# Where the first up pair's weight parts are made and how the last squares are added, in a fused hybrid decoder layer on one core

## The chip, the cores and the metric

The kernel runs on one core of one Trainium2 chip. The time is the device time of one launch in microseconds; a kernel is judged by the median of several launches. The profile is one launch taken by the hardware profiler. The engines are named as the profile names them: PE is the matrix engine (PEld its weight loads), DVE the vector engine, ACT the scalar engine, POOL is GpSimd, SP the engine that only issues transfers. "SPq", "ACTq" and "POOLq" are transfers issued from these engines' queues.

## What is computed

One decoder layer over 1024 positions of width 1024, in float32: a norm, two attention branches, a gated merge of the branches, an output product (the mixing layer) with a residual, then a norm and a gated MLP with a short convolution, a residual and a last norm. The parts that matter here:

```python
xn = rmsnorm(x, norm_mix_w[l])
proj = xn @ w_in[l]
...
merged = jax.nn.sigmoid(g_da) * (y_da @ w_br_da[l]) + jax.nn.sigmoid(g_sw) * (y_sw @ w_br_sw[l])
x = x + merged @ w_mix_out[l]
xn = rmsnorm(x, norm_ffn_w[l])
x = x + conv_ffn(xn, w_up[l], conv_w[l], conv_b[l], w_down[l])
```

## The kernel before

**Numbers in two parts.** Every operand of a product is held as a high part (a rounded copy, made on ACT, L252 or L150) and a low part (source minus high part, made on DVE, L254 or L152). A product is three matmuls: high by high, high by low, low by high. So each weight tile of 128 by 1024 costs one load on SP, one cast on ACT and one subtraction on DVE before PE can use it. `raw` (three buffers) takes the loads, `wh` and `wl` (two buffers each) the parts; in the up projection `sh`, `sl` (three each) and `rv` are used beside them.

**Fast products.** The input projection, the mixing layer, the up and the down projection each form a block product by seven half-size products (Strassen's scheme in Winograd's form): P1 to P7 over operands A11, A12, S1 to S4, A22 of the weights and B11, B21, T1 to T4, B22 of the activations. The sums among weights for the mixing layer are made in memory during the input projection: copies on SP and accumulating transfers on POOL, by a generator `sums_of` that is advanced some steps for each of nine weight pairs (L568). After it `sums_up` (L106) does the same for one up pair, j = 1, into the tensor `ud`, in eight steps.

**Attention, then the merge.** The branch outputs lie in the tensor `yd` and the gates' inputs in `gd`. In `rest` (L896) eight rows of `yd` are loaded (`yr`, L909) and cut into parts `yh`, `yl`; then a loop over m = 0 to 7 does one block row of the merge: load two gate rows (`gr`, four buffers, so those of m+2 can be loaded only when those of m are used up), scale them on POOL (L925), take the sigmoid on ACT (L932), run 48 matmuls on PE into `sc` and `g`, multiply on DVE (L941, L943), and add the two branches into `mr[:, m]` on POOL (L951; the last two on DVE). Rows of `mr` are cut into the parts `x` (and `m22`, for B22) by `split` (L966, L967). The order on each engine is made by a scheduler from the order of the code and `issue_after` ties; an engine runs its instructions strictly in that order.

**Splitting in the merge.** The generator `ahead_parts` (L136), advanced twice in each turn of the merge, loads four tiles (half of the mixing weight, and both tiles of the up pair j = 0), makes that pair's sums on DVE, makes high parts on ACT and low parts on DVE, and stores both parts to memory: `md4` for the mixing layer's last stage, `ud0` for the up pair j = 0. They come back later as finished parts: `md4` through `load_halves` (L117) in stage P4, `ud0` through `pre_pair` (L126) after stage P7.

**The mixing layer** (`mix`, L975) runs the stages P1, P2, P5, P6, P3, P7, P4 in two halves each, numbered i = 0 to 13, of 24 matmuls each (L1117). The weights of half i+1 are fetched at half i. After each half the results are added to the residual rows `xm` on DVE, and a table `due` lists, by half, which operations prepare the up projection's activations: scales and casts on ACT, sums and low parts on DVE. It also holds the squares for the second norm: each row is squared on ACT (L1024) into `sqs` or `rv`, and the squares are summed in `rstd` by POOL. The last four go by an accumulating transfer, the others by an addition:

```python
if m > 3 and hf == 0:
    nc.gpsimd.dma_start(a, sq, accum_op=ALU.add)
else:
    nc.gpsimd.tensor_tensor(a, a, sq, ALU.add)
```

**The up projection** (`hidden`, L1157) takes 22 pairs of seven products of 12 matmuls each (L1154). For j = 0 six products come first (B11, T1, B22, T3, T2, B21), then the column sums of `rstd` on PE (L281), the last product (T4), the first two products of j = 1, and the spreading of the norm's factor (L296). `recombine` adds the products up; for a pair whose sums came by `sums_up` its signs differ (`pre`).

Of the kernel before, what the change touches and what calls it, by code (L numbers as in the profile page):

```python
# [27 lines left out]
RAW = 3  # L28
HP, HPB, HR = 7, 13, 11
# [16 lines left out]
class Trunk:  # L46
# [27 lines left out]
    def ahead(self, n):  # L74
        while len(self.wq) < n and self.wsrc and (self.wsrc[0][1] != "pair" or self.uw):
# [10 lines left out]
            elif nk == "halves":  # L86
                self.wq.append(self.load_halves(src, "raw" if src is self.md4[0] else None))
            else:
                self.wq.append(self.load_w(src, nk, *eng))
# [16 lines left out]
    def sums_up(self):  # L106

        nc, d = self.nc, self.ud
        row = lambda j, r: self.w_up[j].rearrange("p k c -> p (k c)")[:, r * H2:(r + 1) * H2]
        copy = lambda n, src: nc.sync.dma_start(d[:, n], src)  # L110
        add = lambda n, src: nc.gpsimd.dma_start(d[:, n], src, accum_op=ALU.add)
        for f, n, src in ((copy, 0, row(1 + NF, 0)), (copy, 2, row(1 + NF, 0)), (add, 0, row(1 + NF, 1)), (add, 2, row(1, 0)),
                          (copy, 1, d[:, 0]), (add, 1, row(1, 0)), (copy, 3, d[:, 1]), (add, 3, row(1, 1))):
            f(n, src)
            yield

    def load_halves(self, src, tag=None, pool=None, tags=("wh", "wl"), shape=[P, KC, P]):  # L117

        r = []
        for d, t in zip(src, tags):  # L120
            x = self.tl(self.wp, shape, tag, F32R, bufs=RAW) if tag else self.tl(pool or self.wp, shape, t, F32R)
            self.sync = self.nc.sync.dma_start(x.bitcast(F32).rearrange("p a k c -> p (a k c)" if len(shape) == 4 else "p k c -> p (k c)"), d).ins
            r.append(x)
        return r

    def pre_pair(self):  # L126

        w, shape = {}, [P, 2, 4, P]
        for i, n in enumerate((("A11", "A12"), ("S1", "S2"), ("S3", "S4"))):
            hi, lo = self.load_halves(self.ud0[i], None, self.uw if i else self.wp, ("sh", "sl") if i else ("wh", "wl"), shape)  # L130
            w.update({name: (hi[:, a], lo[:, a]) for a, name in enumerate(n)})
        x, = self.load_halves(self.ud0[3], None, self.uw, ("sh",), shape)
        w["A22"] = x[:, 0], x[:, 1]
        return w

    def ahead_parts(self, pool):  # L136


        nc, tt = self.nc, self.nc.vector.tensor_tensor
        late = []  # L140

        def load(src):
            t = self.tl(pool, [P, T], "yr")
            nc.sync.dma_start(t.rearrange("p (m k c) -> p m k c", m=src.shape[1], k=src.shape[2]) if len(src.shape) == 4 else t.rearrange("p (k c) -> p k c", k=KC), src)
            return t

        def cut(t, hi, lo, n=T):
            h = self.tl(pool, [P, T], "yh", F32R, bufs=1)
            x, r = t[:, T - n:], h[:, :n]
            nc.scalar.copy(r, x)  # L150
            nc.scalar.dma_start(hi, r.bitcast(F32))
            tt(x.bitcast(F32R), x, r.bitcast(F32), ALU.subtract)  # L152
            late.append(lambda: nc.sync.dma_start(lo, x))

        def sums(g, v):
            q = lambda t, i: t[:, i * H2:(i + 1) * H2]
            a, b = (self.tl(pool, [P, T], "yr") for _ in range(2))
            tt(q(a, 0), q(v, 0), q(v, 1), ALU.add)
            tt(q(a, 1), q(a, 0), q(g, 0), ALU.subtract)
            tt(q(b, 0), q(g, 0), q(v, 0), ALU.subtract)  # L160
# [20 lines left out]
        for m in range(KC):  # L181
            steps = plan(m)
            while late:
                late.pop(0)()
# [1377 lines left out]
```

## Time and profile before

| | |
|---|---|
| median of 3 runs | 1345.48 us (1343.78 to 1346.31) |
| the profiled execution | 1345.87 us, its span 1344.0 us |
| PE busy | 1311.3 us (98%), granted clock 0.986 |
| DVE, ACT, POOL busy | 1069.9, 639.9, 502.3 us |
| stages, from the trace | projection to 240 us, attention to 497, merge to 608, mixing to 686, up projection to 1121, down to the end |

A busy share is a mean over stages with different limits, so the stages are looked at one by one: how long PE stood still in each, at what clock it ran, and what ended its waits. Durations of single instructions are in microseconds (ns where marked); "idle before" in brackets is the time that the engine stood still ahead of the row and what ended it.

### The profile page before, as it was taken

The numbers are of one execution on the slowest core, as the hardware profiler recorded it, in microseconds if no ns is written. First come the engines' busy times: TensorE is split into PE (matmuls) and PEld (weight loads), VectorE is DVE, ScalarE is ACT, GpSimd is POOL, SyncE is SP. The second block draws the span as 40 slices with busy tenths as digits, with TensorE's granted clock in tenths as the row PEclk, the third lists the DMA queues.
The fourth block names the chain that finished last, engine by engine and source line by source line (L and its number), as shares of the span: only waits on it lengthen the run. The fifth ranks groups of instructions, "written<-read, shape, count | busy, mean of one in ns | idle before, by whom it ended". The sixth has DMA issues, their size and how long they took to land.

```text
span 1344.0 us, 17329 instructions
## 1 busy us (share of the span) xinstructions
PE 1311.3 (98%) x6162; PEld 1090.2 (81%) x6162; DVE 1069.9 (80%) x1516; ACT 639.9 (48%) x1010; POOL 502.3 (37%) x399
## 2 busy tenths in 40 slices
PE   9999999999999999799998999999999999999997
PEld 7888888888888878677876888888888888888886
DVE  8846684388898964557787999999999999896865
ACT  9432232376676764234654443343334335554643
POOL 0448762010101006653244666676657642000002
PEclk9999999999999999898998999999999999999998
DMA  8357776966552157759594534663636237953534
GB/s 296 130 165 214 225 213 163 276 178 172 157 134 89 61 178 255 221 191 317 155 287 154 182 126 131 169 203 101 201 121 153 86 102 244 319 197 114 167 96 145
DMA packets 87318, 238.21 MB, mean 177 GB/s; under 512 B 9665, under 2 KB 17473, under 8 KB 86977
## 3 DMA queue, kind: packets, MB, share of 16 engines
q1 hardware_dynamic: 64848, 193.86, 43.2%
q0 software_dynamic: 8640, 23.07, 10.2%
q10 hardware_dynamic: 13744, 20.19, 4.1%
q8 instruction: 48, 0.79, 0.3%
q14 instruction: 38, 0.30, 0.1%
HBM read 176.27 MB, written 88.08 MB: 197 GB/s over the span
## 4 chain that ended last, share of the span: by engine, by line
PE 85%; DMA 5%; POOL 4%; issue 3%; ACT 1%; DVE 1%; SPq 1%; POOLq 0%; ACTq 0%; DVEq 0%
PE t L1154 43%; PE y L1375 9%; PE d L1375 7%; PE m L1117 5%; PE g L273 3%; PE g L274 3%; PE g L275 3%; PE sc L766 3%; POOL gr L925 2%; DMA gr<-gd 2%; POOL mr L951 1%; DMA rstd<-rv 1%; PE t L782 1%; PE t L885 1%; PE sc L854 1%
## 5 line engine op out<-in xcount | busy, mean ns | idle before, releaser
L254 DVE TENSOR_TENSOR wl<-raw,wh 128x1024 fp32r<-128x1024 f32 (+2 forms) x89 | 94.3, 1060 | 56.2 <-ACT wh L252 46.6
L252 ACT CAST wh<-raw 128x1024 fp32r<-128x1024 f32 (+2 forms) x89 | 78.3, 881 | 88.9 <-PE y L1375 47.6
L1154 PE MATMUL t<-T,sh 128*128 128x512 f32 x364 | 113.1, 395 | 0.0
L1305 POOL TENSOR_TENSOR us<-us,rstd 128x1024 f32<-128x1024 f32 x42 | 93.6, 2303 | 50.3 <-DVE us L599 32.5
L290 POOL TENSOR_TENSOR rs<-ms,mhalf 128x8 f32<-128x8 f32 (+2 forms) x9 | 13.3, 1478 | 236.9 <-DVE ms L288 230.7
L217 POOL TENSOR_TENSOR sf<-rv 128x512 f32<-128x512 f32 x29 | 59.5, 2052 | 97.4 <-DMA rv<-in_w_up 51.2
L231 ACT CAST sh<-sf 128x1024 fp32r<-128x1024 f32 x58 | 60.7, 1047 | 67.5 <-PE t L1154 32.7
L1319 ACT ACTIVATE c<-us,vecs 128x1024 f32<-128x1024 f32 x44 | 54.7, 1247 | 70.6 <-POOL us L1305 67.4
L233 DVE TENSOR_TENSOR sl<-sf,sh 128x1024 fp32r<-128x1024 f32 x58 | 78.5, 1354 | 12.0 <-ACT sh L231 11.9
L1154 PE MATMUL t<-x,wh 128*128 128x512 f32 x248 | 82.2, 389 | 0.0
L1154 PEld LDWEIGHTS t<-T,sh 128*128 128x128 f32 x364 | 69.4, 191 | 14.6
L1322 DVE SCALAR_TENSOR_TENSOR c<-us,vecs,c 128x1024 f32<-128x1024 f32 x44 | 73.3, 1698 | 0.1
L273 PE MATMUL g<-xh,wh 128*128 128x512 f32 x176 | 71.1, 404 | 1.4 <-ACT g L695 1.4
L274 PE MATMUL g<-x,wh 128*128 128x512 f32 x176 | 70.5, 400 | 0.0
L275 PE MATMUL g<-xh,wl 128*128 128x512 f32 x176 | 70.3, 399 | 0.0
L1154 PE MATMUL t<-x,sh 128*128 128x512 f32 x212 | 68.7, 392 | 0.0
L1154 PE MATMUL t<-T,sl 128*128 128x512 f32 x176 | 68.5, 389 | 0.0
L233 DVE TENSOR_TENSOR wl<-raw,wh 128x1024 fp32r<-128x1024 f32 x29 | 67.7, 2333 | 0.6
L1321 DVE SCALAR_TENSOR_TENSOR c<-us,vecs,c 128x1024 f32<-128x1024 f32 x44 | 65.0, 1511 | 1.7 <-ACT c L1319 1.7
L1375 PE MATMUL y<-h,wh 128*128 128x512 f32 (+1 forms) x224 | 65.3, 375 | 0.0
L219 POOL TENSOR_TENSOR sf<-raw,rv 128x512 f32<-128x512 f32 x29 | 52.2, 1801 | 34.4 <-DVE sl L233 34.4
L770 DVE CUSTOM_DVE_ANT_0 L<-sc,bias 128x128 f32<-128x128 f32 (+7 forms) x64 | 47.7, 752 | 17.5 <-PE sc L766 14.0
(350 smaller groups left out, 3978.4 us busy)
## 6 DMA issues: line engine op xcount, KB each, us to landing
u<-qd SPq DMA_DIRECT2D x72, 256.0 KB, 6.7
raw<-in_w_in SPq DMA_DIRECT2D x22, 512.0 KB, 5.6
hd<-c SPq DMA_DIRECT2D x22, 512.0 KB, 2.6
sdP<-in_w_down POOLq DMA_DIRECT2D x16, 704.0 KB, 9.2
raw<-in_w_up SPq DMA_DIRECT2D x21, 512.0 KB, 5.4
rv<-in_w_up SPq DMA_DIRECT2D x20, 512.0 KB, 3.8
hc<-hd SPq DMA_DIRECT2D x33, 256.0 KB, 5.1
gr<-gd SPq DMA_DIRECT2D x16, 512.0 KB, 6.1
```

The source lines that it names most:

```text
L233: low = nc.vector.tensor_tensor(lo, src, hi.bitcast(F32), ALU.subtract)
L252: self.hi = nc.scalar.copy(wh, raw)
L254: self.lo = (eng or nc.vector).tensor_tensor(wl, raw, wh.bitcast(F32), ALU.subtract)
L273: nc.tensor.matmul(ps, wh[:, kc + o, :], ah, start=first and n == 0, stop=False)
L274: nc.tensor.matmul(ps, wh[:, kc + o, :], al, start=False, stop=False)
L275: nc.tensor.matmul(ps, wl[:, kc + o, :], ah, start=False, stop=last and n == len(kcs) - 1)
L1117: nc.tensor.matmul(ps, v[:, m % 2 * 4 + k, :], x, start=start and k == j == 0, stop=k == 3 and j == 2, skip_group_check=True)
L1154: nc.tensor.matmul(ps, (ah, ah, al)[p][:, k, :], (bh, bl, bh)[p], start=first and n == p == 0, stop=last and p == 2 and n == len(ks) - 1, ...
L1305: i = (nc.vector if m % NF == 0 else nc.gpsimd).tensor_tensor(us[:, 2:], us[:, 2:], self.rstd, ALU.mult)
L1321: nc.vector.scalar_tensor_tensor(c, us[:, 1:T + 1], cw[1], c, ALU.mult, ALU.add)
L1322: nc.vector.scalar_tensor_tensor(c, us[:, 0:T], cw[0], c, ALU.mult, ALU.add)
L1375: nc.tensor.matmul(ps, v[:, k - k0, :], x, start=start and k == i == 0, stop=k == HK - 1 and i == 2, skip_group_check=True)
```

## The change

The merge no longer makes any parts: `ahead_parts`, `load_halves` and `pre_pair` go, with the tensors `md4` and `ud0`. Stage P4's weights are loaded raw and cut like all others. The first up pair, j = 0, now gets its sums as j = 1 did, by `sums_up` during the input projection (NPRE = 2: sixteen steps in place of eight, and 6, 6, 6, then 5 steps for each weight pair in place of 5 and 4). Its parts are made by `part_pair` in the mixing layer: parts 0 and 1 at i = 8 and 9, part 2 at i = 12, part 3 (A22) as the new operation `y3` in the last entry of `due`. They are put where the merged rows `mr` lay: the pool `mp` is closed after stage P3's split, and `uw` is opened there; B22's parts of the merge and T2 share a new pool `zp`. All squares are added by POOL additions. `recombine` takes its other signs for j < 2.

```diff
+NPRE = 2
-            elif nk == "halves":
-                self.wq.append(self.load_halves(src, "raw" if src is self.md4[0] else None))
...
-        copy = lambda n, src: nc.sync.dma_start(d[:, n], src)
-        add = lambda n, src: nc.gpsimd.dma_start(d[:, n], src, accum_op=ALU.add)
+        copy = lambda n, src: lambda j: nc.sync.dma_start(d[j][:, n], src(j))
+        add = lambda n, o, r: lambda j: nc.gpsimd.dma_start(d[j][:, n], row(j + o, r), accum_op=ALU.add)
+        for step in (copy(0, lambda j: row(j + NF, 0)), copy(2, lambda j: row(j + NF, 0)), add(0, NF, 1), add(2, 0, 0),
+                     copy(1, lambda j: d[j][:, 0]), add(1, 0, 0), copy(3, lambda j: d[j][:, 1]), add(3, 0, 1)):
+            for j in range(NPRE):
+                step(j)
+                yield
...
-    def part_pair(self, src, part):
+    def part_pair(self, src, part, first=False):
-        pool, h, l = (self.uw, "sh", "sl") if part in (1, 2) else (self.wp, "wh", "wl")
+        pool, h, l = (self.uw, "sh", "sl") if part in (1, 2) or first else (self.wp, "wh", "wl")
...
-                if name == "P4":
-                    src.append((self.md4[h], "halves"))
-                    continue
-                    m, a = 2 * h, 4 * (name != "P1")
+                    m, a = 2 * h + 4 * (name == "P4"), 4 * (name != "P1")
...
-                for _ in range(5 if j < 4 else 4):
+                for _ in range(6 if j < 3 else 5):
...
-                ahead = self.ahead_parts(yrp)
-                    with tc.issue_after(self.sync):
-                        next(ahead)
-                    with tc.issue_after(self.last.ins):
-                        next(ahead)
...
-            if m > 3 and hf == 0:
-                nc.gpsimd.dma_start(a, sq, accum_op=ALU.add)
-            else:
-                nc.gpsimd.tensor_tensor(a, a, sq, ALU.add)
+            nc.gpsimd.tensor_tensor(a, a, sq, ALU.add)
...
+        def last_part(k):
+            with tc.issue_after(tails[0]), tc.issue_after(tails[1]):
+                w0.update(self.part_pair(pair, k))
+            tails[:] = self.lo.ins, self.hi.ins
...
-                        w = self.next_w(3 if i > 9 else 2)
-                    if i < 11:
+                        w = self.next_w()
+                    if i < 13:
                         tails[:] = self.lo.ins, self.hi.ins
...
                             elif n == 4:
                                 split_m("T4", 4, 0)
+                                mctx.close()
+                                uw = self.hctx.enter_context(tc.tile_pool(name="uw", bufs=3, side="right", reuse_waits="tile"))
+                                pair = self.wsrc.pop([e[1] for e in self.wsrc].index("pair"))[0]
+                    if n == 4 or i == 12:
+                        self.uw = uw
+                        with tc.issue_after(tails[1] if i == 12 else self.hi.ins), tc.issue_after(tails[0] if i == 12 else self.lo.ins):
+                            w0.update(self.part_pair(pair, {8: 0, 9: 1, 12: 2}[i], True))
...
-                    w0 = self.pre_pair()
-                self.recombine(ps, us, tp, 2, self.lo.ins if j == NF - 1 else None, j == 1)
+                self.recombine(ps, us, tp, 2, self.lo.ins if j == NF - 1 else None, j < NPRE)
```

Three places in the order of instructions. The first is SP's queue where the merge begins: the branch rows `yr`, the gate rows `gr` and the branch weights `raw`. Before:

```order
L242 DMA raw_5209<-in_w_br 128x1024
L909 DMA yr_4955<-yd 128x1024
L909 DMA yr_4995<-yd 128x1024
L909 DMA yr_5029<-yd 128x1024
L909 DMA yr_5069<-yd 128x1024
L909 DMA yr_5103<-yd 128x1024
L909 DMA yr_5109<-yd 128x1024
L909 DMA yr_5115<-yd 128x1024
L909 DMA yr_5121<-yd 128x1024
L924 DMA gr_5142<-gd 128x1024
L924 DMA gr_5146<-gd 128x1024
```

and with the change:

```order
L168 DMA raw_5215<-in_w_br 128x1024
L846 DMA gr_5148<-gd 128x1024
L846 DMA gr_5152<-gd 128x1024
L830 DMA yr_5106<-yd 128x1024
L830 DMA yr_5112<-yd 128x1024
L830 DMA yr_5118<-yd 128x1024
L830 DMA yr_5124<-yd 128x1024
L846 DMA gr_5221<-gd 128x1024
L846 DMA gr_5225<-gd 128x1024
L168 DMA raw_5288<-in_w_br 128x1024
```

The first four branch rows moved ahead of these weights, and the first two gate rows (m = 0) ahead of the last four branch rows; those of m = 1 follow these, and no loads of `ahead_parts` come behind them.

The second place is POOL at the end of the mixing layer, where the last squares (`rv`) are added into `rstd` and the operands of T4 into `xm`. Before:

```order
L1027 TENSOR_TENSOR rstd<-rstd,rv_6361 128x512
L1025 DMA rstd<-rv_6362 128x512
L1045 TENSOR_TENSOR xm_5804<-xm_5804,xm_5808 128x512
L1025 DMA rstd<-rv_6362 128x512
L1045 TENSOR_TENSOR xm_5805<-xm_5805,xm_5809 128x512
L1025 DMA rstd<-rv_6361 128x512
L1045 TENSOR_TENSOR xm_5806<-xm_5806,xm_5810 128x512
L1025 DMA rstd<-rv_6361 128x512
L1045 TENSOR_TENSOR xm_5807<-xm_5807,xm_5811 128x512
```

and with the change:

```order
L942 TENSOR_TENSOR rstd<-rstd,rv_6334 128x512 x2
L960 TENSOR_TENSOR xm_5766<-xm_5766,xm_5770 128x512
L960 TENSOR_TENSOR xm_5767<-xm_5767,xm_5771 128x512
L942 TENSOR_TENSOR rstd<-rstd,rv_6333 128x512
L960 TENSOR_TENSOR xm_5768<-xm_5768,xm_5772 128x512
L942 TENSOR_TENSOR rstd<-rstd,rv_6333 128x512
L960 TENSOR_TENSOR xm_5769<-xm_5769,xm_5773 128x512
```

The four transfers became additions; two squares now stand ahead of all T4 sums, and the last still ahead of one.

The third place is DVE from stage P3's second half on: `wl` are the weights' low parts for the next half, `xm` the additions of a half's results. Before:

```order
L1142 TENSOR_TENSOR xm_5805<-xm_5805,m_5828 128x512
L254 TENSOR_TENSOR wl_6219<-raw_6215,wh_6217 128x1024
L1142 TENSOR_TENSOR xm_5806<-xm_5806,m_5829 128x512
L1142 TENSOR_TENSOR xm_5807<-xm_5807,m_5830 128x512
L254 TENSOR_TENSOR wl_6266<-raw_6262,wh_6264 128x1024
L1142 TENSOR_TENSOR xm_5808<-xm_5808,m_5823 128x512
```

and with the change:

```order
L1067 TENSOR_TENSOR xm_5767<-xm_5767,m_5790 128x512
L128 TENSOR_TENSOR sl_6154<-raw_6150,sh_6152 128x1024
L180 TENSOR_TENSOR wl_6191<-raw_6187,wh_6189 128x1024
L128 TENSOR_TENSOR sl_6197<-raw_6193,sh_6195 128x1024
L1067 TENSOR_TENSOR xm_5768<-xm_5768,m_5791 128x512
L1067 TENSOR_TENSOR xm_5769<-xm_5769,m_5792 128x512
L180 TENSOR_TENSOR wl_6236<-raw_6232,wh_6234 128x1024
L1067 TENSOR_TENSOR xm_5770<-xm_5770,m_5785 128x512
```

Two low parts of the first up pair (`sl`) came in, one on each side of the weights for i = 10; further down two more `wl` (stage P4's), one `sl` and one half-size `wl` (A22) are new.

104 lines of the change are left out of this document (19 added, 85 removed), and 2 rows, old and new, of the table due.

## The prediction

> **What bounds the kernel now.** The profiled execution took 1345.87 us with a span of 1344.0; it lies 0.4 above the median. I read first the busy time of each engine by stretches: PE is what the end waits for, so a stage with PE busy throughout at full clock can gain nothing. Columns: from:to, length, busy time and instructions of PE, PEld, DVE, ACT, POOL, then PE's granted clock, the DMA engines' busy share, GB/s.
>
> ```profile
> 497.00:608.00 111.00, 98.47 (x414) 80.12 (x413) 56.83 (x63) 44.88 (x50) 65.04 (x29) 0.95 0.69 225
> 608.00:690.00 82.00, 82.00 (x352) 67.54 (x352) 66.71 (x88) 48.39 (x77) 26.43 (x24) 0.97 0.83 253
> 690.00:730.00 40.00, 32.34 (x132) 26.43 (x131) 25.06 (x29) 14.63 (x23) 19.61 (x17) 0.83 0.69 217
> 730.00:1121.00 391.00, 391.00 (x1727) 323.76 (x1726) 380.85 (x332) 159.11 (x169) 243.73 (x171) 1.00 0.45 138
> ```
>
> The rows are the merge, the mixing layer, the transition to the up projection, and the up projection. The last has no gap and clock 1.00, so it gives PE's pace: 391.00 / 1727 = 0.2264 us a matmul. Against that pace the merge's 414 matmuls need 93.7 us of 98.47 busy (4.7 lost to a lowered clock), and it stood still for 12.5 more. The mixing layer needs 79.7 of 82.00 (2.3 lost). Next, which waits on PE ended these stops (start, duration, engine, line, operation; idle before in brackets), from PE's timeline:
>
> ```profile
> 554.42 0.50 PE L273 MATMUL g<-yh,wh 128*128 128x512 f32 x1 [2.51 <-DVE gr L943]
> 567.35 0.80 PE L275 MATMUL sc<-yh,wl 128*128 128x512 f32 x1 [5.10 <-DVE wl L254]
> 607.58 0.80 PE L1117 MATMUL m<-x,wl 128*128 128x512 f32 x1 [4.92 <-DVE wl L254]
> ```
>
> 2.51 + 5.10 + 4.92 = 12.53: all of the merge's idle time. Merge and mixing together thus hold 12.5 + 4.7 + 2.3 = 19.5 us that a perfect feed would give back. The transition is read from the chain of waits (start, duration, what):
>
> ```profile
> 678.05 6.64 DMA sl<-ud
> 684.72 8.44 DMA rstd<-rv
> 697.55 2.22 DMA rstd<-rv
> 703.73 2.21 DMA rstd<-rv
> 708.93 3.22 DMA rstd<-rv
> 712.20 3.58 PE t L281 x16
> 725.75 0.87 PE t L296 x8
> ```
>
> The column sums (L281) wait for four accumulating transfers in a row. Full-size products in 690 to 730 are 132 less 24 small ones, 108 x 0.2264 = 24.5 us; the column sums at full clock take some 1.7 (an estimate: about half of the 3.58 that they took at a clock near one half) and the spreading 0.9. So 27 of 40 us are work and 13 are lost. In all 19.5 + 13 = 32.5 us can be had, no more.
>
> **Change, merge.** What goes: L150's casts on ACT, L152's cuts on DVE, four sums on DVE, four loads and seven stores of whole or half tiles. I first ask which ring sets the merge's pace. On POOL:
>
> ```profile
> 561.84 2.35 POOL L951 TENSOR_TENSOR mr<-gr,gr 128x1024 f32<-128x1024 f32 x1
> 567.93 5.71 POOL L925 TENSOR_TENSOR gr<-gr,rstd 128x1024 f32<-128x1024 f32 x2 [1.08 <-DMA gr<-gd]
> 573.61 3.37 POOL L951 TENSOR_TENSOR mr<-gr,gr 128x1024 f32<-128x1024 f32 x1
> 586.75 2.40 POOL L925 TENSOR_TENSOR gr<-gr,rstd 128x1024 f32<-128x1024 f32 x1 [3.24 <-DMA gr<-gd]
> 589.10 2.40 POOL L951 TENSOR_TENSOR mr<-gr,gr 128x1024 f32<-128x1024 f32 x1
> 591.53 0.32 SPq L924 DMA_DIRECT2D gr<-gd  x1
> 591.94 0.38 SPq L153 DMA_DIRECT2D ud<-yr  x1
> 592.41 0.38 SPq L924 DMA_DIRECT2D gr<-gd  x1
> 601.71 2.36 POOL L925 TENSOR_TENSOR gr<-gr,rstd 128x1024 f32<-128x1024 f32 x1 [3.61 <-DMA gr<-gd]
> L152 DVE TENSOR_TENSOR yr<-yr,yh 128x1024 fp32r<-128x1024 f32 (+1 forms) x6 | 11.6, 1940 | 5.4 <-ACT yh L150 5.4
> ```
>
> With four `gr` buffers a row's `mr` sum frees the next pair of loads, which then feed two POOL multiplications and a sum. From 564.19 (end of one `mr`) to 576.98 (the next but one's) the ring turned in 12.8 us, with PE needing 48 x 0.2264 = 10.9. It also waited for the second gate row of a pair: 601.71 is 9.3 after its issue at 592.41, behind a store `ud<-yr` of the merge's own parts; the first landed near 595.7, 4.2 after its issue. Without those stores I put the turn at 4.2 for the load, the second row landing while the first is multiplied, 2.4 + 2.4 for the two multiplications and 2.4 for the sum, 11.4, and 0.5 to 1 where a `wl` cut on DVE lengthens the sum as at 573.61 (3.37 for 2.35): about 12. That is still 1.1 over PE's 10.9 for each of some six turns, 6.6 us. Against that stands a lead: the first gate rows are now ahead of four `yr` rows on SP (the first place in the order), four loads, which I take as 6 us. The lead about covers the lag. The two long stops on `wl` go by themselves: the weights' cut no longer stands behind L152 cuts of 1.94 each, nor (at 567.35) behind the `x` part of the row before. I take 16.5 of the 19.5; the bounds are 3 (only the 2.51 stop and its clock, if the gate rows still bind) and 19.5.
>
> **Change, squares and transition.** Four accumulating transfers, 8.44 + 2.22 + 2.21 + 3.22 with waits of 3 to 4.4 between them, become four additions:
>
> ```profile
> L1027 POOL TENSOR_TENSOR rstd<-rstd,sqs 128x512 f32<-128x512 f32 x8 | 12.3, 1544 | 24.4 <-ACT sqs L1142 24.3
> L1025 POOL DMA_DIRECT2D rstd<-rv x4 | 4.2, 1045 | 11.3 <-issue 6.9 <-ACT rv L1142 4.4
> L1045 POOL TENSOR_TENSOR xm<-xm,xm 128x512 f32<-128x512 f32 x4 | 6.4, 1600 | 5.3 <-DVE T L1142 5.3
> 694.01 0.50 PE L1154 MATMUL t<-B,sl 128*128 128x512 f32 x1 [1.82 <-DMA sl<-ud]
> ```
>
> Four at 1.54 and four `xm` sums at 1.60 are 12.6 us of POOL work. The last square's `xm` was ready by the transfer's issue, and POOL's first `xm` sum began at 691.52 on DVE's result; with squares two ahead of the sums and two among them, the last square lies behind at most three sums: 691.5 + 3 x 1.6 + 4 x 1.54 is 702.5. PE's six products of j = 0 end 72 x 0.2264 = 16.3 after the mixing layer's last product, 686.1 + 16.3 = 702.4. So the column sums wait for next to nothing; the 5.83 us that PE now stands still ahead of them go. Also the 1.82 stop goes, since the first pair's parts are now made from the eighth half on and no seven-tile load is due. Of the 13 I keep 4 for T4's low parts, which still come after the `xm` sums, and for a clock lowered once: 9 gained, bounds 3 and 13.
>
> The clock: at 696 to 697, after that stop of 1.82, it was 0.50.
>
> ```profile
> 696.00:697.00 1.00, 1.00 (x4) 0.73 (x3) 0.75 (x1) 1.00 (x3) 0.00 (x0) 0.50 1.03 387
> ```
>
> [...]
>
> **Change, mixing layer.** Added on DVE: five cuts of 128x1024 (two `wl` of P4; parts 0, 1 and 2 of the pair) and one of half that size (A22), 5.5 in all. Added on ACT: as many casts.
>
> ```profile
> L254 DVE TENSOR_TENSOR wl<-raw,wh 128x1024 fp32r<-128x1024 f32 (+2 forms) x89 | 94.3, 1060 | 56.2 <-ACT wh L252 46.6
> L233 DVE TENSOR_TENSOR wl<-raw,wh 128x1024 fp32r<-128x1024 f32 x29 | 67.7, 2333 | 0.6
> 650.00:660.00 10.00, 10.00 (x46) 8.29 (x45) 9.06 (x13) 5.52 (x9) 0.00 (x0) 1.00 0.36 120
> 660.00:670.00 10.00, 10.00 (x45) 8.29 (x45) 6.62 (x7) 6.78 (x11) 4.65 (x3) 1.00 0.49 156
> 670.00:680.00 10.00, 10.00 (x45) 8.26 (x44) 9.99 (x12) 6.65 (x13) 6.00 (x5) 1.00 0.97 265
> 680.00:690.00 10.00, 10.00 (x46) 8.27 (x45) 10.00 (x14) 9.18 (x16) 3.94 (x4) 1.00 1.04 348
> ```
>
> At 1.06 each the cuts are 5.8 us, at 2.33 (beside POOL's work and transfers, as in the up projection) 12.8. DVE has 0.94 + 3.38 = 4.3 us free from 650 to 690, so it ends 1.5 to 8.5 later than now. The products of j = 0 in their order give some 4 us of room: T3's low part ends near 690 and is needed by the fourth product, 686.1 + 3 x 12 x 0.2264 = 694.3. With cuts near 1.4 (7.7 us, lag 3.4) the room holds. A second wait is on `raw`: three buffers now also take the pair's parts, so stage P7's second weights can load only when part 0 is cut; I allow 2 us of PE waiting for both. Bounds 0 and 8. Fewer bytes move where the DMA share is 0.97 and 1.04: finished parts came as high and low, now each tile comes once.
>
> **Change, input projection.** Eight more steps of `sums_up`: four more copies on SP, four more accumulations on POOL.
>
> ```profile
> 65.00:240.00 175.00, 175.00 (x774) 144.91 (x773) 109.97 (x117) 49.56 (x59) 100.61 (x72) 1.00 0.70 202
> 153.75 8.04 SPq L98 DMA_DIRECT2D mdP<-mdP  x4
> ```
>
> PE is busy for all 175 us while SP was held 8.04 us by four such copies; POOL is 57% busy and DMA 70%. The cover is the weights' two-deep lookahead. I take 0.5 us, bounds 0 and 8 (one such block uncovered).
>
> **Sum.** -16.5 - 9 + 2 + 0.5 = -23.0; 1345.87 - 23.0 = 1322.9, forecast 1323. Its own range is 1315 to 1331 (the merge 4 worse, the transition 3 worse; or all of merge and transition, with no price in the mixing layer).
>
> **Rivals.**
>
> *The gate rows still bind.* If the second row of a pair lands 9 us after its issue even with no store between, as at 601.71, the ring is 9 + 2.4 + 2.4 = 13.8, no shorter than before's 12.8, and the merge gains 3 only: -3 - 9 + 2.5 = -9.5, 1336. For it: these loads waited as well where only few stores were about; against it: the pair at 567.93 waited 1.08 only. Chance 0.10.
>
> *DVE's tail is stretched by POOL's squares.* Additions on POOL replace transfers just where DVE is busy 10.00 of 10.
>
> ```profile
> 566.08 1.22 DVE L254 TENSOR_TENSOR wl<-raw,wh 128x1024 fp32r<-128x1024 f32 x1
> 581.12 2.39 POOL L925 TENSOR_TENSOR gr<-gr,rstd 128x1024 f32<-128x1024 f32 x1 [2.86 <-DMA gr<-gd]
> 581.27 3.33 DVE L152 TENSOR_TENSOR yr<-yr,yh 128x1024 fp32r<-128x1024 f32 x1
> ```
>
> DVE's cut beside a POOL operation took 3.33 and ended 1.09 after it; alone the same shape took 1.22. So DVE can lose the whole POOL time: 4 x 1.54 = 6.2 on top of the lag of 3.4, 9.6, which is 5.4 over the room of 4.2; with 2 for the clock 7.4: -23 + 7.4 = -15.6, 1330. Chance 0.13. [...]
>
> *The pair's parts can't wait* (the end on the other side). Every added cut takes 2.33 and each stands on DVE ahead of `xm` additions that free PE's results and prepare T3 and T4: 12.8 late, of which no more than 4.3 is covered. From stage P3 on PE then waits for `wl`, `T3`, `T4` in turn, 8.5 at each of two places and the clock lowered after them (some 3): about +20, the transition gains nothing, the merge its 16.5, and the input projection shows its 3 or more: 1345.87 + 20 + 3 - 16.5 = 1352. It decides once the lag is over some 7 us. For it: DVE's 9.99 and 10.00; against it: POOL is idle in 650 to 660, where cuts were near 1.1. Chance 0.10.
>
> *The squares don't come sooner.* POOL's additions stand behind `xm` sums that wait for their own operands, so the column sums still come at 712: the transition gains 3 or 4 instead of 9: 1328. Chance 0.05.
>
> **How the numbers follow.** Forecast 0.62. About 0.2% (2.7 us) is what a measurement tells from no change. All but the third rival are faster, 0.90; I move 0.03 of the first to no change (its ring with a full lag besides), and 0.02 of the third: faster 0.87, same 0.05, slower 0.08. The range 1310 to 1340 holds the forecast nearly whole and the three faster rivals; what is out is the third and the ends.
>
> **What would show it.** In the merge, `mr` ends no more than 12 us apart, and no PE stop on `wl` (L254's successor); if the stops move to DVE's `gr` products, the ring binds. At the transition, column sums without a wait; a wait on a low part of T3 or T4 instead shows the tail of DVE. In the mixing layer, added cuts near 1.1 to 1.4 and no PE stop at L1117; above 2 the third rival. In the input projection PE busy throughout. The prediction is wrong if the merge keeps over 8 us of stops, or if PE waits over 5 us between 608 and the column sums.

## The result, and the profile after

The changed kernel takes 1332.19 us (median of 4 runs, 1330.49 to 1334.75) against 1345.89 for the kernel before in the same comparison: a ratio of 0.9892 with an interval of 0.9853 to 0.993. In a second comparison it took 1332.65 against 1343.73, 0.9924 (0.9909 to 0.9939). It is faster by 11 to 14 us, where 23 were forecast.

The busy line of the page after, and then its stages by stretches (columns as in the prediction); the limits are the merge's first product, the mixing layer's first, the up projection's first and the end of the spreading.

```profile
PE 1305.2 (98%) x6162; PEld 1082.2 (81%) x6162; DVE 1078.2 (81%) x1512; ACT 635.8 (48%) x1010; POOL 509.5 (38%) x403
```

```profile
504.00:591.00 87.00, 87.00 (x385) 72.05 (x384) 55.18 (x54) 33.01 (x37) 58.76 (x27) 1.00 0.59 176
591.00:669.00 78.00, 76.85 (x338) 62.91 (x336) 60.67 (x76) 47.25 (x71) 22.30 (x20) 1.00 0.76 227
669.00:705.00 36.00, 30.32 (x135) 23.49 (x134) 34.12 (x38) 17.69 (x30) 19.61 (x16) 0.95 0.57 183
```

The merge has no gap left: 385 matmuls in 87 us at full clock. What still stops PE is in its timeline, the same view as the three stops of 2.51, 5.10 and 4.92 before:

```profile
237.19 0.47 PE L199 MATMUL g<-xh,wh 128*128 128x512 f32 x1 [1.09 <-DVE u L518]
663.32 0.73 PE L1043 MATMUL m<-x,wh 128*128 128x512 f32 x2 [0.74 <-DVE xm L1067]
672.63 0.74 PE L1079 MATMUL t<-T,sh 128*128 128x512 f32 x2 [0.46 <-DVE xm L1067]
676.80 0.70 PE L1079 MATMUL t<-B,sh 128*128 128x512 f32 x2 [1.11 <-ACT x L1067]
686.06 0.59 PE L1079 MATMUL t<-z,sh 128*128 128x512 f32 x1 [1.98 <-DVE z L1067]
704.02 1.09 PE L222 MATMUL t<-ident,rs 128*128 128x128 f32 x8 [1.89 <-POOL rs L216]
1101.12 0.62 PE L1300 MATMUL y<-sh,wh 128*128 128x512 f32 x2
1108.39 0.70 PE L1300 MATMUL y<-sh,wh 128*128 128x512 f32 x2 [3.02 <-DVE us L520]
```

Small stops along the transition, and one of 3.02 at a place that had none before: the down projection's first products (`y`, from 1101.12 on), which wait for VectorE's last sums of the up projection. With five marks of PE's timeline (first product of the merge, of the up projection, end of the spreading, first product of the down projection, end of the span) the 15.2 us between the two profiled spans fall into:

| stretch | before | after | difference | forecast |
|---|---|---|---|---|
| start to the merge | 502.8 | 504.2 | +1.4 | +0.5 |
| merge and mixing layer | 183.3 | 164.9 | -18.4 | -16.5 + 2 |
| transition, to the end of the spreading | 40.5 | 36.0 | -4.5 | -9 |
| up projection, to the first down product | 394.3 | 396.0 | +1.7 | 0 |
| down projection | 223.1 | 227.7 | +4.6 | 0 |
| sum | 1344.0 | 1328.8 | -15.2 | -23.0 |

By these two profiles the merge gave more than forecast (the old merge and mixing layer took 181.0 and 181.1 in two other profiles below, by which it gave 16); half of the transition's gain is missing, and 6 us are given back in the two projections behind it, which no term of the sum had.

### The profile page after: what moved, and what is told of

Its sections match the earlier page's. It is cut to its first block, busy times and chain, and to the rows that moved or that the text cites. A ratio compares the mean times of both kernels' runs of the same rounds, so it can differ in the third digit from the quotient of the medians.

```text
span 1328.8 us, 17311 instructions
## 1 busy us (share of the span) xinstructions
PE 1305.2 (98%) x6162; PEld 1082.2 (81%) x6162; DVE 1078.2 (81%) x1512; ACT 635.8 (48%) x1010; POOL 509.5 (38%) x403
## 4 chain that ended last, share of the span: by engine, by line
PE 67%; DVE 14%; issue 7%; DMA 5%; POOL 4%; ACT 3%; SPq 0%; POOLq 0%; ACTq 0%; DVEq 0%
PE t L1079 19%; PE y L1300 9%; PE d L1300 7%; PE g L199 4%; PE g L201 4%; PE g L200 4%; PE m L1043 4%; PE sc L687 3%; DVE wl L159 2%; DVE c L1246 2%; DVE c L1247 1%; PE t L703 1%; POOL us L502 1%; DMA ud<-in_w_up 1%; PE sc L201 1%
## 5 line engine op out<-in xcount | busy, mean ns | idle before, releaser
L180 DVE TENSOR_TENSOR wl<-raw,wh 128x1024 fp32r<-128x1024 f32 (+2 forms) x91 | 109.9, 1209 | 49.7 <-ACT wh L178 41.5
L159 DVE TENSOR_TENSOR sl<-sf,sh 128x1024 fp32r<-128x1024 f32 x58 | 74.1, 1277 | 14.8 <-ACT sh L157 14.8
L670 POOL MEMSET aT<- 128x128 f32 x32 | 6.2, 206 | 141.8 <-PE t L716 100.0
L1043 PE MATMUL m<-x,wh 128*128 128x512 f32 x192 | 59.0, 390 | 0.7 <-DVE xm L1067 0.7
L692 ACT ACTIVATE L<-L,sm 128x128 f32<-128x128 f32 (+7 forms) x64 | 49.6, 779 | 20.2 <-DVE sm L691 17.5
```

The costliest lines, as they stand in the source:

```text
L159: low = nc.vector.tensor_tensor(lo, src, hi.bitcast(F32), ALU.subtract)
L180: self.lo = (eng or nc.vector).tensor_tensor(wl, raw, wh.bitcast(F32), ALU.subtract)
L1043: nc.tensor.matmul(ps, v[:, m % 2 * 4 + k, :], x, start=start and k == j == 0, stop=k == 3 and j == 2, skip_group_check=True)
```

## The experiments

The kernel before ran beside every experiment (medians 1343.09, 1342.69 and 1343.73 us); the changed kernel, where times are compared, is 1332.65.

**Which half of the change gives what: the kernel before with the merge emptied.** The loop no longer advances the generator. This kernel leaves the parts out: `md4` and `ud0` name one stored tile of branch parts (`one`), which is loaded where the parts were, so its result is not the layer's. From the edit:

```diff
-                ahead = self.ahead_parts(yrp)
+                nc.scalar.dma_start(self.one, parts[0][0].bitcast(F32))
+                ahead = iter(int, 1)
```

> The kernel before without any splitting in the merge: no loads, sums, casts, cuts and stores of the mixing layer's last weights and of the first up pair there; where these parts are loaded later, one stored tile of branch parts is loaded in place of each, so the weights of that stage and of that pair are not the reference's. By the prediction's first term (16.5) the time from the merge's start to the mixing layer's end falls from 183.4 to about 167; by the changed kernel's trace (164.9 with the added cuts in the mixing layer) to 163 to 165, and the total by 15 to 19, the transition to the up projection staying as long as before. Rival (what freed the merge is the order of SP's loads, not the work removed): under 8 us of it.

1328.2 us, ratio 0.9888 (0.9873 to 0.9903): 14.5 less than the kernel before. From the merge's first product to the up projection's first it took 164.2 us, against 183.3 and 164.9. So without the parts the merge and the mixing layer gain what the change gains, and the cuts that the change puts into the mixing layer cost it only 0.7 us. The rival (the order of SP's loads) does not fall by this run, since here too the first two gate rows came ahead of the branch rows:

```profile
483.13 5.09 SPq L926 DMA_DIRECT2D gr<-gd  x2
495.79 4.20 SPq L910 DMA_DIRECT2D yr<-yd  x4
```

What each is worth is told by the run with the gate rows behind the branch rows, further down.

The transition keeps its old form and length (40.1):

```profile
691.98 3.57 PE L281 MATMUL t<-ones,rstd 128*128 128x1 f32 x16 [9.10 <-DMA rstd<-rv]
```

**The kernel before with the squares alone.**

```diff
-            if m > 3 and hf == 0:
-                nc.gpsimd.dma_start(a, sq, accum_op=ALU.add)
-            else:
-                nc.gpsimd.tensor_tensor(a, a, sq, ALU.add)
+            nc.gpsimd.tensor_tensor(a, a, sq, ALU.add)
```

> The kernel before with its last four squares added by GpSimd and nothing else changed. By the prediction's second term, which gave most of 9 us to the squares: 6 to 9 us faster, the column sums no longer waiting 5.83. Rival, from the run of the changed kernel with transfers (no slower in all, since VectorE's lag took it back at the down projection's start): the column sums come sooner, but under 3 us of it is left at the end.

1335.73, ratio 0.994 (0.9925 to 0.9955): 8.0 less. The rival falls. The transition went from 40.5 to 28.6 us, and the column sums wait for nothing. PE's and POOL's timelines of this run:

```profile
702.38 1.84 PE L281 MATMUL t<-ones,rstd 128*128 128x1 f32 x16
```

```profile
699.79 1.75 POOL L1024 TENSOR_TENSOR rstd<-rstd,rv 128x512 f32<-128x512 f32 x1
```

The last square ends at 701.54, a microsecond before the sums. So the two halves of the change, each by itself on the kernel before, give 14.5 and 8.0, together 22.5, about the forecast; done together they give 11 to 14. (Neither half has the added sums of the input projection or the added cuts of the mixing layer.)

**The changed kernel with transfers for the squares again** (the same edit, reversed).

> The changed kernel with its last four squares added by accumulating transfers as before. By the prediction's second term the squares are worth 9 us: about 1341. By the changed kernel's trace the transition gained 4.5 us in all, so 3 to 6 us slower, about 1336, with the column sums again waiting for the transfers. By the rival (GpSimd's additions stretch VectorE's cuts by as much as they save) no difference within 2 us.

1330.85: no difference. The column sums again wait, 4.60, and the spreading starts 36.3 us after the first up product instead of 34.9; but the stop at the down projection's start is gone:

```profile
696.95 3.43 PE L207 MATMUL t<-ones,rstd 128*128 128x1 f32 x16 [4.60 <-DMA rstd<-rv]
1105.58 0.61 PE L1303 MATMUL y<-sh,wh 128*128 128x512 f32 x2
```

The squares that gave 8 us alone are worth nothing here: the transition is only 1.3 us longer than the changed kernel's (37.3 for 36.0), and what PE loses there, it does not lose at the end of the up projection. This points to VectorE, which runs beside PE through all of it.

**A lag put in by hand:** the kernel before, with VectorE held up in the fourth up pair.

```diff
+                if j == 3:
+                    for _ in range(6):
+                        nc.vector.tensor_scalar(us[0][:, 2:], us[0][:, 2:], 1.0, None, ALU.mult)
```

> The kernel before with six additional VectorE operations (a multiplication of one row of 128x1024 by 1, some 0.6 to 1.2 us each, 4 to 7 in all) after the fourth up pair, j = 3. Theory L: VectorE has no time to catch up in the up projection (380.85 us busy of 391), so the matrix engine stops at the down projection's first products for about what was added: 4 to 8 us slower. Theory R: absorbed within a few pairs, under 1 us.

1346.81, ratio 1.0022 (1.0011 to 1.0034). The six operations took 8.07 us. Against the spreading's end, VectorE came 5.1 us later with the sums of the pair behind them, 5.0 with those of j = 20, and PE stopped some 340 us behind the place:

```profile
1124.96 0.69 PE L1378 MATMUL y<-sh,wh 128*128 128x512 f32 x2 [1.24 <-DVE us L600]
```

So this lag of VectorE in the up projection isn't made up. It costs less than its length, 3.7 for 8.07: 3 went into VectorE's idle time, and the kernel before had a little to spare. The stop of 1.24 is not all of the cost: the up projection itself took 396.3 us for 394.3, with stops of 0.41 and 0.61 on VectorE's sum `u`.

**The order of the first rows.** The changed kernel's VectorE does nothing for 4 us at the start of the up projection:

```profile
708.82 1.34 DVE L159 TENSOR_TENSOR sl<-sf,sh 128x1024 fp32r<-128x1024 f32 x1 [4.09 <-ACT sh L157]
712.93 3.44 DVE L1230 TENSOR_TENSOR us<-us,rstd 128x1024 f32<-128x1024 f32 x2
```

The cut of pair j = 2 waits there for a cast that waits for GpSimd's sums, and the multiplication by the norm's factor stands behind it.

```diff
-                        w, ps = ready[j + 1] = self.next_w(), {}
+                        w, ps = ready[j + 1] = self.next_w(2 if j else 1), {}
...
-                        nc.scalar.copy(self.rstd[:, hf * H2:(hf + 1) * H2], sp)
+                        spr = nc.scalar.copy(self.rstd[:, hf * H2:(hf + 1) * H2], sp)
+                    with tc.issue_after(spr.ins):
+                        self.ahead(1)
```

> The changed kernel with one order changed: the parts of pair j = 2 are made behind the copies of the norm's factor, so that ScalarE copies the factor and VectorE multiplies the first rows by it before it cuts j = 2 (in the changed kernel the copies stood behind a cast that waited for GpSimd's sums of j = 2). Theory L: VectorE needs some 395 us from its first row multiplication to the sums that the down projection's first products wait for, in every trace so far (396.7, 395.3, 394.9, 395.7, 396.3), so a start 4 to 5 us sooner after the spreading takes the 3.02 stop and its lowered clock away: 3 to 5 us less than the changed kernel. Rival: the chain's length is not fixed, pair j = 2 comes late for the matrix engine instead, and the time is within 1 us of the changed kernel's.

1332.4, no difference, and the stop is 3.03. The order is as meant (the multiplication comes 1.1 us after the spreading instead of 7.8), but what it passed on VectorE now comes behind it: the sums of pair j = 1 end 22.3 us after the spreading instead of 24.3. The expectation took one instruction for the state of the engine. What the runs below follow better is how far VectorE is behind PE with the same work done.

**The last part of the first pair cut early** (parts of two entries of `due`).

```diff
-(13, 0): "l30 l31"
+(13, 0): "l30 l31 y3"
...
-hb3 c33 a43 lb3 y3 "
+hb3 c33 a43 lb3 "
```

> Only the place of the last part of the first up pair (A22: its cast and its cut) differs from the changed kernel: it is cut after the first block of the mixing layer's last half instead of behind all operands but T4's. Theory L (a lag carried along): the raw buffer comes free some 25 us earlier, so the third load of pair j = 1 is not the last thing before the column sums' mean; the 1.89 stop ahead of the spreading goes, VectorE's first row multiplication comes at about 707 instead of 712.93, and the stop of 3.02 us at the down projection's first products, 400 us later, with its lowered clock, goes too: 5 to 6.5 us less than the changed kernel, about 1326. Theory R (the stop at the down projection is made there, by its own loads): only the 1.89 goes, about 1330, and the 3.02 stays.

1332.07, no difference: the stop before the spreading is gone, the 4.10 of idle time on VectorE and the stop at the down projection (3.04) are not. Of what theory L foretold only the first part came. The lag does not come from that raw buffer.

**The tail on VectorE.** Four sums and four squares move from GpSimd to VectorE (the other squares stay):

```diff
+            if m > 3 and hf == 0:
+                vec(tt, a, a, sq, ALU.add)
...
-"a4": lambda k: nc.gpsimd.tensor_tensor(col(k, 0), col(k, 0), col(k + 4, 1), ALU.add)
+"a4": lambda k: add(col(k, 0), col(k + 4, 1))
```

> The four sums for T4 and the four last squares are added on VectorE instead of GpSimd. Theory S (VectorE's cuts at the end of the mixing layer are stretched by GpSimd beside them, 1.7 for 0.68): eight additions of 0.68 come in, some 10 us of stretch go, VectorE's tail ends about 5 us earlier, the 1.98 stop on T2's low parts and the lowered clock go: 3 to 7 us less than the changed kernel. Rival (the stretch has another cause, the transfers of that time): the cuts stay at 1.7, the tail gets 5 us longer, and the kernel 3 to 5 us slower.

1327.14, ratio 0.9876 (0.9858 to 0.9895): 5 less than the changed kernel, though VectorE has more to do. Groups by line on VectorE from the first up product on (count, busy us, mean ns), first of the changed kernel (669 to 694), then of this run (672.5 to 697):

```profile
L1067 DVE SCALAR_TENSOR_TENSOR x<-xm,ms,x 128x512 fp32r<-128x512 f32 x4 | 6.0, 1512 | 0.0
L1067 DVE TENSOR_TENSOR z<-xm,z 128x512 fp32r<-128x512 f32 x4 | 4.7, 1217 | 0.0
L1067 DVE TENSOR_TENSOR xm<-xm,c 128x512 f32<-128x512 f32 x2 | 2.9, 1513 | 0.0
```

```profile
L1070 DVE SCALAR_TENSOR_TENSOR x<-xm,ms,x 128x512 fp32r<-128x512 f32 x4 | 3.0, 743 | 0.0
L1070 DVE TENSOR_TENSOR z<-xm,z 128x512 fp32r<-128x512 f32 x4 | 2.6, 679 | 0.0
L1070 DVE TENSOR_TENSOR xm<-xm,c 128x512 f32<-128x512 f32 x2 | 1.3, 678 | 0.0
```

In this run GpSimd does nothing from 677.0 to 694.4, and the same operations take about half the time. The transition falls from 36.0 to 32.0 us.

**Where the added sums are made.** In seven profiles with the change's early part the merge starts at 504.2 to 509.1 (mean 507.0), in four without it at 501.9 to 503.8 (mean 502.7): 4.3 us. Two other places were tried. First, more steps early in the input projection:

```diff
-                for _ in range(6 if j < 3 else 5):
+                for _ in range((7, 7, 6, 6, 6, 5, 4, 4, 3)[j]):
```

> The changed kernel with the 48 steps of sums in memory spread over the nine weight pairs of the input projection as 7, 7, 6, 6, 6, 5, 4, 4, 3 instead of 6, 6, 6 and then 5. In four traces with the change the merge starts at 504.2, 507.5, 507.6 and 509.1, in two without it at 502.8 and 501.9, and GpSimd is busy 13 to 14 us of 20 before the projection's end instead of 7. Theory T (the added steps are late at the projection's end, where GpSimd's row work waits behind their transfers): the stop of 1 to 2 us on the first attention weights goes and the merge starts near 503: 2 to 4 us less. Rival (it is the mere number of transfers): the stops move to an earlier pair and the merge starts at 504 to 509 as before.

1332.72, no difference; the merge starts at 504.3, and the stop at the projection's end (at 237 to 240 in the changed kernel's profiles) has moved to an earlier pair:

```profile
122.51 0.50 PE L1079 MATMUL t<-xh,wh 128*128 128x512 f32 x1 [0.67 <-ACT wh L157]
124.08 0.51 PE L1079 MATMUL t<-xh,wl 128*128 128x512 f32 x1 [0.84 <-DVE wl L159]
```

Then the eight steps of j = 0 in the attention, one after each pair of query blocks of the second and third head:

```diff
+                            if u in (1, 2):
+                                with tc.issue_after(self.sync), tc.issue_after(self.sum):
+                                    next(sums)
```

> The changed kernel with the eight added sum steps (pair j = 0) taken out of the input projection, which gets the kernel before's 40 steps at its rates, and put into the attention, one step a pair of query blocks, where GpSimd is busy 10 to 12 us of 100. Theory T (the eight steps cost the input projection 1.4 to 7 us, by stops on late parts): the merge starts at 502 to 503 instead of 504 to 509, 2 to 5 us less than the changed kernel. Rival (the spread of the merge's start has nothing to do with them, or the attention loses as much to their transfers): 504 or later, within 1 us of the changed kernel.

1333.26, no difference; the merge starts at 505.1. The input projection has no stop but one of 0.60 at its start, but the attention has new ones, such as

```profile
484.78 1.19 PE L810 MATMUL t<-aT,v 128*128 128x512 f32 x4 [1.29 <-DVE aT L804]
487.25 0.50 PE L199 MATMUL g<-xh,wh 128*128 128x512 f32 x1 [0.84 <-ACT g L620]
```

In both the time is as the rival has it: by the medians the steps cost about the same wherever they were put. The merge's start varies too much from launch to launch for one profile each (504.3 and 505.1, for a mean of 507.0) to say more, and what exactly the steps disturb is open.

**The lead of the gate rows.** The first two are loaded behind all eight branch rows again:

```diff
-                        nc.sync.dma_start(r, self.yd[c])
+                        rows = nc.sync.dma_start(r, self.yd[c])
...
-                        nc.sync.dma_start(g, self.gd[8 * br + m])
+                        with tc.issue_after(rows.ins) if m == 0 else nullcontext():
+                            nc.sync.dma_start(g, self.gd[8 * br + m])
```

> The changed kernel with the gate rows of m = 0 loaded behind all eight branch rows, as in the kernel before. By the prediction the merge lives on a lead of some 6 us against a ring that lags 1.1 us a row: without it the matrix engine would stop in the merge's second half, 4 to 6 us slower from the merge's start to the end of the mixing layer (164.9 us now). Rival (the ring without stores is faster than the matrix engine's 10.9 us a row): no stop, 165 us, within 1 us of the changed kernel.

1338.41, ratio 0.9965 (0.9952 to 0.9978): 5.8 slower than the changed kernel, and 170.7 instead of 164.9 from the merge's start to the mixing layer's end. Its PE stops at the end of the merge and in the mixing layer's first products:

```profile
590.72 0.50 PE L199 MATMUL g<-yh,wh 128*128 128x512 f32 x1 [0.70 <-DVE gr L862]
598.01 0.50 PE L1044 MATMUL m<-x,wl 128*128 128x512 f32 x1 [1.09 <-DVE wl L180]
602.24 0.73 PE L1044 MATMUL m<-x,wh 128*128 128x512 f32 x2 [1.67 <-DVE gr L864]
```

The lead is worth what was worked out for it. It does not come from an edit meant for it: the scheduler put these loads first. With the run above this parts the gain: of the 18.4 us of merge and mixing layer 12.6 (183.3 less 170.7) come without the lead, from the removed work (10.3 if the old merge is taken at 181.0), and 5.8 with it.

**The changed kernel again, and four edits together** (sums in the attention, the tail on VectorE, A22 early, the first rows first).

> The changed kernel once more, beside the same runs of the kernel before as the others of this call: 0.985 to 0.993 of the kernel before. Its merge starts anywhere from 504 to 509 if that start varies from launch to launch, and the stop of 3.0 at the down projection's start comes again.

1332.65, ratio 0.9924 (0.9909 to 0.9939); merge start 506.2, stop 3.01.

> Four edits together: the added sum steps in the attention, T4's sums and the last squares on VectorE, A22 cut early, and pair j = 2 made behind the copies of the norm's factor. If VectorE's lag sets the up projection's end, their gains add: 2 to 5 (merge's start), about 4 (VectorE's tail shorter) and 1 to 2 (its idle time of 4 us before j = 2): 7 to 10 us under the changed kernel, 1321 to 1325. If the lag is not what binds, only the merge's start and the shorter tail remain: 1326 to 1329.

1324.69, ratio 0.9856 (0.9838 to 0.9875): 8 less than the changed kernel, the fastest of all. The stop at the down projection is down to 0.90:

```profile
1102.52 0.70 PE L1309 MATMUL y<-sh,wh 128*128 128x512 f32 x2 [0.90 <-DVE us L521]
```

The merge's start (506.8) gained nothing; the transition is 31.0. The time lies where the expectation put it if VectorE's lag binds (1321 to 1325), but its interval overlaps that of the tail alone, so what the other three edits add is not settled by the times.

The runs side by side. "Behind" is how long after the spreading's end VectorE ends its sum `us<-t,u` for pair j = 1; "stop" is PE's wait in the down projection's first products, "down" the time from the first of them to the end.

| kernel | transition | behind | stop | down | median |
|---|---|---|---|---|---|
| before | 40.5 | 18.3 | none | 223.1 | 1343 to 1346 |
| merge emptied | 40.1 | 18.2 | none | 223.0 | 1328.2 |
| changed, squares by transfer | 37.3 | 18.1 | none | 223.2 | 1330.9 |
| four edits | 31.0 | 21.4 | 0.90 | 225.5 | 1324.7 |
| changed, first rows first | 35.4 | 22.3 | 3.03 | 227.8 | 1332.4 |
| before, squares alone | 28.6 | 22.5 | 1.22 | 225.4 | 1335.7 |
| changed, tail on VectorE | 32.0 | 23.3 | 3.01 | 228.1 | 1327.1 |
| changed | 36.0 | 24.3 | 3.02 | 227.7 | 1332.2 |

With VectorE 18 us behind there is no stop, with 21 or more there is one, and the down projection is 2 to 5 us longer (the stop, and in the changed kernel's profile 3.4 us at a granted clock of 0.50 behind it, from 1109.6 on). The other five runs of the changed kernel fit: 23.6 to 24.3 behind, stops of 3.01 to 3.04, down 226.1 to 228.0. VectorE has little time to catch up: in the kernel before its sums for j = 20 end 365.2 us after those for j = 1, 19.2 us a pair, where PE needs 84 x 0.2264 = 19.0. The changed kernel's VectorE is 6.1 us later than that of the kernel before at j = 1, and still 4.7 later at j = 20 (3.3 in its second profile).

Why is the stop nearly the same, 3.0, from 22.3 to 24.3? In every run that has one, VectorE ends the last pair's `us<-t,u` 6.8 to 7.1 us after the down projection's first product, in the runs without one 3.6 to 4.2. A lag beyond that shows earlier, as small stops of PE inside the up projection on VectorE's sum `u`, in the profile of the changed kernel:

```profile
879.53 0.72 PE L1079 MATMUL t<-z,sh 128*128 128x512 f32 x2 [0.33 <-DVE u L515]
1032.77 0.73 PE L1079 MATMUL t<-z,sh 128*128 128x512 f32 x2 [0.24 <-DVE u L515]
```

That the stop is 1.2 with the squares alone, at 22.5, comes from another sum waited for. The last pair ends with two sums on VectorE, 1.8 us apart. In the changed kernel, shown here, PE waited for the second (L520), with the squares alone for the first (L600 there). Why the two kernels differ in that stays open.

```profile
1105.77 0.68 DVE L521 TENSOR_TENSOR us<-u,t 128x512 f32<-128x512 f32 x1
1107.56 0.68 DVE L520 TENSOR_TENSOR us<-t,u 128x512 f32<-128x512 f32 x1
```

## Why the prediction came out as it did

The sign was right, the time lies inside the range (1310 to 1340), and the size was off: 11 to 14 us for 23.

**Merge, -16.5: right in mechanism, too small.** The stops on `wl` went as argued. The ring turned in 10.8 us (the `mr` sums end at 518.50, 529.32, 540.23, 551.07) and only later in 13.1 and 11.8; "about 12" for all was too long for the first rows, and the lead covered the rest. Merge and mixing layer together gave 18.4 of the 19.5 to be had, or 16 by the two other profiles of the old merge. That the lead counts is shown by its removal (5.8 for an estimated 6); without it the `mr` sums end 11.7 to 13.7 apart. (The prediction calls the sum that ends at 576.98 "the next but one's"; POOL's rows show it to be the next one's, and the 12.8 for a turn stands.)

```profile
516.10 2.40 POOL L871 TENSOR_TENSOR mr<-gr,gr 128x1024 f32<-128x1024 f32 x1 [0.87 <-ACT wh L178]
526.92 2.40 POOL L871 TENSOR_TENSOR mr<-gr,gr 128x1024 f32<-128x1024 f32 x1
537.82 2.41 POOL L871 TENSOR_TENSOR mr<-gr,gr 128x1024 f32<-128x1024 f32 x1
548.68 2.39 POOL L871 TENSOR_TENSOR mr<-gr,gr 128x1024 f32<-128x1024 f32 x1
```

**Mixing layer, +2: right up to its last product.** The cuts took 1.27 (`wl`) and 1.22 (`sl`) there, near the 1.4 taken, and the layer paid 0.7.

**Squares and transition, -9: right where it stood alone, not beside the moved cuts.** On the kernel before the squares end at 701.5 (forecast 702.5), the column sums start at 702.4 (forecast 702.4), and 8.0 us are left. That the times agree so well is partly luck: counted from the first up product, which came 1.4 sooner in that run, the column sums start at 17.6 for a forecast 16.3. Beside the moved cuts the transition gained 4.5. The step that failed is "With cuts near 1.4 (7.7 us, lag 3.4) the room holds", and the second rival says why: VectorE's tail *is* stretched by POOL's additions, from 0.68 to 1.2 and 1.5 us an operation, so that T2's low parts came late (the 1.98 stop); T4's came in time. That rival was priced at 7.4; the transition is 7.3 longer in the changed kernel than in the kernel before with the squares alone (35.97 less 28.64). That these two agree is luck in part: with the eight additions off GpSimd the transition was only 4.0 shorter (VectorE then made them itself, in 5.3 us), and 1.89 of the 7.3 is the stop ahead of the spreading, which no term had. It was not a rival beside the forecast, then, but happened together with the larger gain in the merge.

**Input projection, +0.5: too small.** 1.4 in the profiled run, 4.3 as a mean over profiles. The row of 175 us busy in 175 showed that PE had no stop; it did not show how little its weights had to spare. The bounds (0 to 8) held.

**What no term had: the up projection is not a wall of PE alone.** The prediction read its row (PE busy 391.00 of 391.00, clock 1.00) as PE being the bound there and put nothing on it. VectorE's 380.85 in the same row was the warning: VectorE ran the same stretch with 10 us free, a little slower than PE a pair, on a head start. Time that PE gains ahead of that stage, and VectorE does not, uses the head start up and comes back as waits, most of it where the stage ends: 1.7 in the up projection and 4.6 in the down projection. The lag put in by hand shows it; the table above agrees. It is only one reason why the halves give 22.5 apart and less together. Against their own profiles the changed kernel's transition is 7.3 longer, its down projection 2.3 (227.7 for 225.4), and it has the added sums (1.4 to 4.3) and cuts (0.7) that neither half has: 12 to 15 by single profiles, where the medians miss 9 to 11.

The clock term was left small, and rightly. The 2 us that the second rival takes for the clock, and the some 3 of the third, are the author's estimates, and no run shows them by themselves; what the changed kernel's trace shows in their place is one stretch of the transition at a granted clock of 0.50, from 686.3 to 689.7, or 1.7 us lost. In the traces of the kernel before and of the changed kernel every stretch at 0.50 but the last, which runs to the span's end, took 3.4, 6.8 or 10.2 us, and within each trace they begin whole multiples of 3.413 us apart. Laid out in that step, up to 9 us before their ends, the two traces have seven steps at full clock in which PE stood still for 1.82 us or more, each followed by one at 0.50; in the other steps at full clock PE stood still for 1.26 us or less, and none of them was. From run to run a stop's length alone does not tell it: the 1.98 stop at 686 brought 3.4 us at 0.50 in the changed kernel, the 1.95 stop at the same place none in the run with the sums early (the next low-part product takes 0.39 us there, 0.63 in the changed kernel); the 1.98 stop at 239 brought a mean clock of 0.83 from 236 to 246 in the second run of the changed kernel, the 1.96 stop at the same place 1.00 in the run with A22 early. And in the run with the tail on VectorE the clock was 0.50 from 694 to 696, behind the column sums, 1.84 us of 128x1 products, with PE idle for only 0.05 us from 688 to 694.

## What to carry to other kernels

Two engines can both be near the bound of one stage; look at the second one's busy time, and at how far it runs behind, before counting on a gain that only brings the first one there sooner. Gains that are worked out one by one need not add up when one engine, here VectorE, is asked for in both: try each half alone on the old kernel, and the sum against the whole. A queue's order that a scheduler changes by the way (the gate rows ahead of the branch rows) was worth 5.8 of the 18.4 us of merge and mixing layer here, and it came along in the test of the half alone as well: look at the order of every run before calling its edit the cause.

## What the runs showed of the hardware

In these runs VectorE operations with both inputs in SBUF took about twice as long beside GpSimd additions: 1.22 to 1.51 us on average for 0.68 to 0.74 in the two lists of groups. In the changed kernel's transition those that began inside an addition took 1.75 to 1.80 each, about as long as the addition (1.72), such as two `z` cuts beside one of the squares:

```profile
684.26 3.44 DVE L1067 TENSOR_TENSOR z<-xm,z 128x512 fp32r<-128x512 f32 x2
685.42 1.72 POOL L942 TENSOR_TENSOR rstd<-rstd,rv 128x512 f32<-128x512 f32 x1
```

Those with one input in PSUM were not stretched: of the sums `us<-u,t` at L517, where `t` is a product's bank, 24 of the changed kernel's began inside a GpSimd TENSOR_TENSOR and took 0.69 us (0.686 to 0.692), as did the 4 that ran beside no GpSimd operation (0.676 to 0.689).

```profile
744.91 0.69 DVE L517 TENSOR_TENSOR us<-u,t 128x512 f32<-128x512 f32 x1
744.60 1.30 POOL L146 TENSOR_TENSOR sf<-raw,sf 128x512 f32<-128x512 f32 x1
```

The consequence was not expected: moving eight additions onto the engine that was already full made it finish sooner (T4's low parts end 21.8 us after the first up product instead of 26.0), and the kernel 5 us faster.
